# Gates by tanh instead of sigmoid, residual rows and channel norm moved to later steps, and a last LayerNorm shared by three engines, in a hybrid decoder layer

## The chip, the cores and the metric

One core of a Trainium2 chip runs the whole layer in one launch. The metric is the device time of that launch in microseconds (us). A run of the kernel before has a median of 1742.73 us over three runs (1742.01 to 1743.32).

The engines are named as in the profile: PE is the matrix engine (PEld its weight loads), DVE the vector engine, ACT the scalar engine, POOL the GpSimd engine, and SP the engine whose queue issues every DMA of this kernel (SPq). Each engine works through its own instructions in order and waits on the others by semaphores.

## The reference

A decoder layer on 256 tokens of width 2048, in float32:

```
x = LN1(alpha*x + 0.5*swiglu_ffn1(x))              # D_FF = 5632
u = x @ w_in + b_in                                # q 1024 | k 128 | v 128 | conv a 1024 | conv gate 1024
attn = sliding-window attention with sinks(q, k, v)   # 16 heads of 64, window 128
h = a * sigmoid(gate)
h = causal depthwise conv(h, 31 taps) + dw_b
conv = silu(LN_channels(h))
x = LN2(alpha*x + concat(attn, conv) @ w_out + b_out)
x = LN3(alpha*x + 0.5*swiglu_ffn2(x))
```

## The kernel before

Every matmul is done three times with split operands: a weight tile `raw` is rounded to `hi` by ACT (L113), and `lo = raw - hi` is made by DVE, in the middle of the program by POOL (L115). PE then adds `hi*hi`, `hi*lo` and `lo*hi` (L387 to L389). The class `Steps` streams the weights: `load` issues DMAs into four `raw` buffers, `split` makes `hi` and `lo` up to seven tiles ahead of PE, and `step()`, called after each bit of matmul work, runs the small jobs that are due. `st.at(delay, work, after)` puts a job on that list, so that the program order on each engine is set by these delays. `psA` has two PSUM buffers of two banks (tag `gu`) and `psB` four of one bank (tag `acc`).

The program runs FFN 1, the mixer, and FFN 2.

- **FFN** (`ffn`, L491): gate and up products by `token_group`, silu on ACT (L507), a transpose on DVE (L515), a split, and the down projection by `tokens_by` (L459). `tokens_by` goes through four column chunks `c` of 512 for two token blocks `b` of 128. `evacuate` (L262) adds a finished chunk to the residual `xt` on DVE (L265) and takes its statistics (L269). In the last six steps block 0 runs ahead: it is finished and normalised while PE still works for block 1.
- **Mixer** (`mixer`, L571): the input projection makes eight conv pairs (`c` in `ORDER`) and the queries (`q`). For a conv pair, `glu` (L660) takes the sigmoid of the gate on ACT (L663) and multiplies on DVE (L664) into `hc`. The 31 taps of the depthwise conv are DVE instructions (L655), started by one on ACT (L651); they accumulate in PSUM and end in `cv`. For each query tile, `attend` (L674) runs scores on PE (L680 to L684), maxima on DVE (L698 to L705), exponentials on ACT (L711, L715), the sum and its reciprocal on DVE (L718, L719), the division on ACT (L725), transposes on PE (L731), values on PE (L744) and the split of the result (L749 on ACT, L750 on DVE).
- **Residual rows** (`residuals`, L336): LayerNorm's gain and bias for the residual are applied to `xt` in four chunks. `get` issues the DMAs of the row vectors (L253). Two steps later ACT multiplies the bias row by alpha (L352), and the following steps hold the rest: DVE's L356, and L354, L360 and L361 on POOL in the mixer, on DVE in FFN 2.
- **Channel norm** (`channel_norm`, L779): when the conv is done, `conv_end` puts the transposes of `cv` (L785) for block 0, and a step later for block 1, into PE's queue, among the first half of the output projection. Then come the norm on DVE, transposes back (L803), silu on ACT (L808) and a split (L813, L814). The second half of the output projection needs these results.
- **The last norm** (`norm_to_rows`, L367): on DVE alone. Four instructions subtract the mean and multiply by the gain (L374), put between the short instructions of a reciprocal square root (`rsqrt`, L274: three rounds of L288 and L289), and four multiply by it and add the bias (L382). Each chunk is then stored (L563).

Of the kernel before, what the change touches and what calls it, by code (L numbers as in the profile page):

```python
# [9 lines left out]
F32 = mybir.dt.float32  # L10
# [3 lines left out]
AF = mybir.ActivationFunctionType  # L14
ALU = mybir.AluOpType
# [3 lines left out]
P = 128  # L19
D = 2048  # L20
S = 256
# [5 lines left out]
NC_ = D // 512  # L27
# [16 lines left out]
CONV_AT = (1, 3, 1)  # L44
# [135 lines left out]
def hybrid_layer(  # L180
# [3 lines left out]
    nc = tc.nc  # L184
# [5 lines left out]
    psA = ctx.enter_context(tc.tile_pool(name="psA", bufs=2, space=PSUM))  # L190
# [24 lines left out]
    xt = act.tile([P, 2, D], F32, tag="xt", name="xt")  # L215
# [21 lines left out]
    def load_constants():  # L237
# [5 lines left out]
        )  # L243
        nc.gpsimd.tensor_scalar(out=nsink, in0=psink, scalar1=-1.0, scalar2=None, op0=ALU.mult)

    def load_tokens(b):
        nc.sync.dma_start(xt[:, b], x[b * P : (b + 1) * P, :])
        st.at(4, lambda: nc.scalar.mul(xt[:, b], xt[:, b], ALPHA))
# [10 lines left out]
        if waiting:  # L259
            waiting.pop(0)()  # L260

    def evacuate(ps, b, c, factor, stats):  # L262

        y = xt[:, b, c * 512 : (c + 1) * 512]
        nc.vector.scalar_tensor_tensor(out=y, in0=ps, scalar=factor, in1=y, op0=ALU.mult, op1=ALU.add)  # L265
# [70 lines left out]
    def residuals(par, row, more, eng, start, every):  # L336

        def scale():
            for b in range(2):
                nc.vector.tensor_scalar(  # L340
                    out=par[:, b, 3:4], in0=par[:, b, 2:3], scalar1=ALPHA, scalar2=None, op0=ALU.mult
                )

        st.at(start, scale)
        for c in range(NC_):
            at = start + 1 + c * every

            def get(c=c, at=at):
                g, be = row_chunk(row, c, f"rg{row}_{c}"), row_chunk(row + 1, c, f"rb{row}_{c}")
                bo = row_chunk(more, c, f"ro{row}_{c}") if more is not None else None  # L350
                ys = [xt[:, b, c * 512 : (c + 1) * 512] for b in range(2)]
                work = [lambda: nc.scalar.mul(be, be, ALPHA)]  # L352
                if more is not None:
                    work.append(lambda: eng.tensor_tensor(out=be, in0=be, in1=bo, op=ALU.add))  # L354
                for b in range(2):
                    work.append(lambda b=b: nc.vector.tensor_scalar(  # L356
                        out=ys[b], in0=ys[b], scalar1=par[:, b, 0:1], scalar2=par[:, b, 3:4],
                        op0=ALU.subtract, op1=ALU.mult,
                    ))
                    work.append(lambda b=b: eng.tensor_tensor(out=ys[b], in0=ys[b], in1=g, op=ALU.mult))  # L360
# [6 lines left out]
    def norm_to_rows(b, stats, par, gb, store):  # L367

        mv, r = par[:, b, 0:2], par[:, b, 2:3]
        nc.vector.bn_aggr(out=mv, in_=stats[b].rearrange("p c s -> p (c s)"))  # L370

        def scaled(c):
            y = xt[:, b, c * 512 : (c + 1) * 512]
            nc.vector.scalar_tensor_tensor(  # L374
                out=y, in0=y, scalar=mv[:, 0:1], in1=gb[c][0], op0=ALU.subtract, op1=ALU.mult
            )

        scaled(0)
        rsqrt(mv[:, 1:2], r, [lambda c=c: scaled(c) for c in range(1, NC_)])
        for c in range(NC_):  # L380
            y = xt[:, b, c * 512 : (c + 1) * 512]
            nc.vector.scalar_tensor_tensor(out=y, in0=y, scalar=r, in1=gb[c][1], op0=ALU.mult, op1=ALU.add)  # L382
            store(b, c, y)


    def mm3(ps, s_hi, s_lo, m_hi, m_lo, start, stop):
# [69 lines left out]
                        evacuate(sums[b], b, c, factor, None)  # L456
                    st.step(1.36)

    def tokens_by(lhs, k0, nk, factor, stats, finish):  # L459

        half = nk // 2
        order = [(c, t) for c in range(NC_) for t in range(half)]
        skew = SKEW if finish is not None else 0
        held, sums = [], {}
        for n, (c, t) in enumerate(order):
            if t == 0:
                sums[c] = [psB.tile([P, 512], F32, tag="acc", name=f"acc{b}") for b in range(2)]
            w = st.take()
            token_mm(sums[c][0], lhs, k0, t, nk, 0, w)
            if t == half - 1:  # L470
                evacuate(sums[c][0], 0, c, factor, stats)
            if n >= len(order) - skew:
                held.append((c, t, w))
            else:
                token_mm(sums[c][1], lhs, k0, t, nk, 1, w)
                st.release()
            if t == half - 1 and not held:
                evacuate(sums[c][1], 1, c, factor, stats)
            if n == len(order) - 1 and skew:
                finish(0)  # L480
            st.step()
        for n, (c, t, w) in enumerate(held):
            token_mm(sums[c][1], lhs, k0, t, nk, 1, w)
            st.release()
            if t == half - 1:
                evacuate(sums[c][1], 1, c, factor, stats)
            if n == skew - 1:
                finish(1)
            st.step()

    def ffn(xc, tag, skew, begun, prepare, finish):  # L491
        with tc.tile_pool(name=f"ffn{tag}", bufs=2) as pool:
            for part, (j0, j1) in enumerate(((0, JA), (JA, JT))):
                n = j1 - j0
# [36 lines left out]
                tokens_by((hh, hl), 0, n, 0.5, stats, (lambda b: finish(b, stats)) if part == 1 else None)  # L531

    def params(name):
        return small.tile([P, 2, 4], F32, tag=name, name=name, bufs=1)
# [16 lines left out]
    x2 = mixer(tc, nc, locals())  # L551


    rows3 = []

    def prepare3(pool):
        for c in range(NC_):
# [7 lines left out]
    ffn(  # L565
        x2, "2", SKEW, lambda: residuals(par2, 3, None, nc.vector, 4, 6), prepare3,
        lambda b, s: norm_to_rows(b, s, par3, rows3, store),
    )


def mixer(tc, nc, env):  # L571
# [6 lines left out]
    with tc.tile_pool(name="mix", bufs=1) as pool:  # L578
# [81 lines left out]
        def glu(i, ps):  # L660
            hc = hcs[i % HB]
            sg = pool.tile([P, S], F32, tag="sg", name="sg", bufs=2)
            nc.scalar.activation(sg, ps[:, S:], AF.Sigmoid, bias=bias[:, 18 + i : 19 + i])  # L663
            nc.vector.scalar_tensor_tensor(  # L664
                out=hc[:, CK - 1 :], in0=ps[:, :S], scalar=bias[:, 10 + i : 11 + i], in1=sg,
                op0=ALU.add, op1=ALU.mult,
            )
            st.vector(0.4, 2.2)
            todo.append((i, hc))
# [244 lines left out]
```

## Time and profile before

| what | value |
|---|---|
| median of three runs | 1742.73 us |
| the profiled execution's own time | 1742.81 us |
| its span, from the first to the last instruction | 1740.9 us |
| mean granted PE clock | 0.997 |
| instructions | 22193 |
| PE busy | 1716.7 us, 99% |
| DVE, ACT, POOL busy | 1197.8, 802.5, 199.7 us |
| HBM traffic over the span | 192 GB/s |

The busy shares are averages over stages with different limits. PE is busy nearly all the time, so that the time can only change where PE stands still or where nothing of PE is left: ahead of its first matmul, in its few waits, and behind its last matmul. A row of the timeline gives the start, the duration, the engine, the line, the operation with its tiles, and, in brackets, how long the engine had stood idle and who released it.

### The profile page before, as it was taken

What the parts mean: (1) busy time and instruction counts of PE and PEld (TensorE: products, weight loads), DVE (VectorE), ACT (ScalarE), POOL (GpSimd) and SP (SyncE); (2) the same over time, 40 slices, a digit from 0 to 9 for tenths busy, and PEclk for the clock granted to TensorE, in tenths of its full rate; (3) what the DMA queues carried; (4) which work ended last, traced back from release to release, by engine and by line L of the source; (5) the groups of instructions that cost most, each with busy time, mean ns of one, the idle gap of its engine ahead of it and who ended that gap; (6) DMA issues with size and microseconds to landing.
All of it is one profiled execution on the core that took longest, in us unless ns stands there. A gap on an engine that the chain in (4) does not pass through costs nothing.

```text
span 1740.9 us, 22193 instructions
## 1 busy us (share of the span) xinstructions
PE 1716.7 (99%) x8198; PEld 1436.1 (82%) x8198; DVE 1197.8 (69%) x1954; ACT 802.5 (46%) x1024; POOL 199.7 (11%) x109
## 2 busy tenths in 40 slices
PE   8999999999999999999999999999999999999996
PEld 6888888888888888898997888888888888888885
DVE  6877776446777765638898588887764467777655
ACT  5544444334444443567565473444443344444430
POOL 0000000000000000178887300000000000000000
PEclk9999999999999999999999999999999999999999
DMA  8865655665565556464554556665556555555761
GB/s 275 282 201 194 192 194 189 198 194 195 192 193 194 193 187 200 146 197 147 175 167 163 194 189 210 208 227 193 192 184 204 193 195 193 192 194 195 232 204 61
DMA packets 96301, 336.42 MB, mean 193 GB/s; under 512 B 11200, under 2 KB 11840, under 8 KB 95936
## 3 DMA queue, kind: packets, MB, share of 16 engines
q1 hardware_dynamic: 96192, 335.00, 58.9%
q8 instruction: 64, 1.05, 0.2%
q14 instruction: 45, 0.37, 0.1%
HBM read 332.86 MB, written 2.10 MB: 192 GB/s over the span
## 4 chain that ended last, share of the span: by engine, by line
PE 88%; DVE 7%; ACT 2%; DMA 1%; issue 1%; POOL 0%; SPq 0%; DVEq 0%; ACTq 0%; POOLq 0%
PE grp L388 18%; PE grp L387 18%; PE grp L389 18%; PE acc L387 10%; PE acc L389 10%; PE acc L388 10%; DVE conv L655 4%; DMA rb<-in_rows 1%; PE grp L406 1%; PE grp L408 0%; PE grp L409 0%; POOL lo L115 0%; DVE xt L356 0%; PE tp L301 0%; ACT pr L725 0%
## 5 line engine op out<-in xcount | busy, mean ns | idle before, releaser
L113 ACT CAST hi<-raw 128x1024 fp32r<-128x1024 f32 (+1 forms) x614 | 639.7, 1047 | 747.8 <-PE grp L389 332.0
L115 DVE TENSOR_TENSOR lo<-raw,hi 128x1024 fp32r<-128x1024 f32 (+1 forms) x542 | 660.7, 1224 | 391.8 <-ACT hi L113 387.4
L387 PE MATMUL grp<-hi,xcat 128*128 128x512 f32 x1392 | 542.9, 390 | 5.7 <-ACT hi L113 5.7
L388 PE MATMUL grp<-lo,xcat 128*128 128x512 f32 x1392 | 542.8, 390 | 0.0
L389 PE MATMUL grp<-hi,xcat 128*128 128x512 f32 x1392 | 542.5, 390 | 0.0
L387 PEld LDWEIGHTS grp<-hi,xcat 128*128 128x128 f32 x1392 | 261.9, 188 | 60.4 <-ACT hi L113 6.0
L388 PEld LDWEIGHTS grp<-lo,xcat 128*128 128x128 f32 x1392 | 261.9, 188 | 55.1 <-DVE lo L115 0.9
L389 PEld LDWEIGHTS grp<-hi,xcat 128*128 128x128 f32 x1392 | 261.9, 188 | 54.4
L387 PE MATMUL acc<-hi,hh 128*128 128x512 f32 x704 | 274.0, 389 | 0.0
L389 PE MATMUL acc<-hi,hl 128*128 128x512 f32 x704 | 273.9, 389 | 0.0
L388 PE MATMUL acc<-lo,hh 128*128 128x512 f32 x704 | 273.9, 389 | 0.0
L115 POOL TENSOR_TENSOR lo<-raw,hi 128x1024 fp32r<-128x1024 f32 x72 | 171.9, 2409 | 772.2 <-ACT hi L113 766.4
L515 DVE STREAM_TRANSPOSE hf<-ht 32x128 f32<-32x128 f32 x704 | 212.7, 302 | 11.3
L389 PEld LDWEIGHTS acc<-hi,hl 128*128 128x128 f32 x704 | 132.2, 188 | 27.5
L387 PEld LDWEIGHTS acc<-hi,hh 128*128 128x128 f32 x704 | 132.2, 188 | 27.3
L388 PEld LDWEIGHTS acc<-lo,hh 128*128 128x128 f32 x704 | 132.2, 188 | 27.3
L655 DVE SCALAR_TENSOR_TENSOR conv<-hc,cw_sb,conv 128x256 f32<-128x256 f32 x232 | 106.9, 486 | 8.7 <-ACT conv L651 3.9
L387 PE MATMUL in_c<-xcat,hi 128*128 128x256 f32 x256 | 73.9, 289 | 0.0
L388 PE MATMUL in_c<-xcat,hi 128*128 128x256 f32 x256 | 72.4, 283 | 0.0
L389 PE MATMUL in_c<-xcat,lo 128*128 128x256 f32 x256 | 72.4, 283 | 0.0
L265 DVE SCALAR_TENSOR_TENSOR xt<-acc,xt 128x512 f32<-128x512 f32 x48 | 33.1, 690 | 55.2 <-PE acc L389 55.2
L507 ACT ACTIVATE sl<-grp 128x256 f32<-128x256 f32 x88 | 32.9, 383 | 48.7 <-PE grp L389 48.7
(118 smaller groups left out, 1058.6 us busy)
## 6 DMA issues: line engine op xcount, KB each, us to landing
raw<-in_wu SPq DMA_DIRECT2D x350, 512.0 KB, 4.6
raw<-in_wd SPq DMA_DIRECT2D x176, 512.0 KB, 4.6
raw<-in_win SPq DMA_DIRECT2D x52, 512.0 KB, 4.2
raw<-in_wout SPq DMA_DIRECT2D x32, 512.0 KB, 4.4
xt<-in_x SPq DMA_DIRECT2D x2, 1024.0 KB, 8.5
rg<-in_rows SPq DMA_DIRECT2D x8, 256.0 KB, 5.3
rb<-in_rows SPq DMA_DIRECT2D x8, 256.0 KB, 6.6
out<-xt SPq DMA_DIRECT2D x8, 256.0 KB, 2.8
```

Source lines behind the costliest of these rows:

```text
L113: nc.scalar.copy(hi, raw)
L115: eng.tensor_tensor(out=lo, in0=raw, in1=hi.bitcast(F32), op=ALU.subtract)
L265: nc.vector.scalar_tensor_tensor(out=y, in0=ps, scalar=factor, in1=y, op0=ALU.mult, op1=ALU.add)
L387: nc.tensor.matmul(ps, s_hi, m_hi, start=start, stop=False)
L388: nc.tensor.matmul(ps, s_hi, m_lo, start=False, stop=False)
L389: nc.tensor.matmul(ps, s_lo, m_hi, start=False, stop=stop)
L406: nc.tensor.matmul(ps, lhs[1][at], w[0][:, n], start=False, stop=k == nk - 1)
L507: nc.scalar.activation(sl, ps[b][:, : JG * P], AF.Silu)
L515: nc.vector.transpose(dst[:, t], src[:, f])
L655: nc.vector.scalar_tensor_tensor(out=acc if k < CK - 1 else cv[:, i], in0=hc[:, k : k + S], scalar=cw_sb[:, i, k : k + 1], in1=acc, op0=AL ...
```

## The change

1. **Gates.** `glu` used one ACT instruction with Sigmoid. It now uses two: Tanh of half the gate, and an Identity that adds 1. The missing factor 0.5 goes into the taps `cw_sb`, and the gate's bias is halved too, both once at the start, on POOL.
2. **Residual rows.** The work on the rows starts five steps after their DMAs are issued, not two. The DMAs stay where they were. This holds for the mixer and for FFN 2.
3. **Channel norm.** Both blocks' channel norms are put one step later.
4. **The last norm.** For token block 1, the chunks 1 to 3 stay in PSUM after `evacuate`, which writes them where it read them; chunks 1 and 2 get a `psA` buffer for that. For block 1, chunk 0 is handled by ACT (subtract the mean, later multiply by the reciprocal root) and POOL (times the gain, later plus the bias). DVE does chunks 1 and 2 as before, and chunk 3 after them. Block 0 is unchanged.

```diff
+        nc.gpsimd.tensor_scalar(out=bias[:, 18:], in0=bias[:, 18:], scalar1=0.5, scalar2=None, op0=ALU.mult)
+        nc.gpsimd.tensor_scalar(out=cw_sb, in0=cw_sb, scalar1=0.5, scalar2=None, op0=ALU.mult)
...
-    def evacuate(ps, b, c, factor, stats):
+    def evacuate(ps, b, c, factor, stats, stay=False):
-        y = xt[:, b, c * 512 : (c + 1) * 512]
-        nc.vector.scalar_tensor_tensor(out=y, in0=ps, scalar=factor, in1=y, op0=ALU.mult, op1=ALU.add)
+        x_ = xt[:, b, c * 512 : (c + 1) * 512]
+        y = ps if stay else x_
+        nc.vector.scalar_tensor_tensor(out=y, in0=ps, scalar=factor, in1=x_, op0=ALU.mult, op1=ALU.add)
...
-                    st.at(2 + n, x_, True)
+                    st.at(5 + n, x_, True)
...
-        scaled(0)
-        rsqrt(mv[:, 1:2], r, [lambda c=c: scaled(c) for c in range(1, NC_)])
-        for c in range(NC_):
-            y = xt[:, b, c * 512 : (c + 1) * 512]
-            nc.vector.scalar_tensor_tensor(out=y, in0=y, scalar=r, in1=gb[c][1], op0=ALU.mult, op1=ALU.add)
-            store(b, c, y)
+        if b == 0:
+            scaled(0)
+            rsqrt(mv[:, 1:2], r, [lambda c=c: scaled(c) for c in range(1, NC_)])
+        else:
+            nc.vector.tensor_scalar(out=par[:, b, 3:4], in0=mv[:, 0:1], scalar1=-1.0, scalar2=None, op0=ALU.mult)
+            nc.scalar.activation(ys[0], ys[0], AF.Identity, bias=par[:, b, 3:4])
+            nc.gpsimd.tensor_tensor(out=ys[0], in0=ys[0], in1=gb[0][0], op=ALU.mult)
+            rsqrt(mv[:, 1:2], r, [lambda c=c: scaled(c) for c in (1, 2)])
+            nc.scalar.mul(ys[0], ys[0], r)
+            nc.gpsimd.tensor_tensor(out=ys[0], in0=ys[0], in1=gb[0][1], op=ALU.add)
+        for c in range(NC_) if b == 0 else (1, 2, 0, 3):
+            if b == 1 and c == 3:
+                scaled(3)
+            if b == 0 or c > 0:
+                nc.vector.scalar_tensor_tensor(
+                    out=ys[c], in0=ins[c], scalar=r, in1=gb[c][1], op0=ALU.mult, op1=ALU.add
+                )
+            store(b, c, ys[c])
...
-            nc.scalar.activation(sg, ps[:, S:], AF.Sigmoid, bias=bias[:, 18 + i : 19 + i])
+            nc.scalar.activation(sg, ps[:, S:], AF.Tanh, bias=bias[:, 18 + i : 19 + i], scale=0.5)
+            nc.scalar.activation(sg, sg, AF.Identity, bias=1.0)
...
-            channel_norm(0)
-            st.at(CONV_AT[2], lambda: channel_norm(1))
+            st.at(1, lambda: channel_norm(0))
+            st.at(1 + CONV_AT[2], lambda: channel_norm(1))
```

The order of ACT's instructions early in the mixer, around the second query tile's exponentials (`pr`), was this in the kernel before; `rb` is the bias row that L352 multiplies, and `ACT_TABLE_LOAD` loads the table of the function that follows:

```order
L113 CAST hi_6181<-raw_6001 128x1024
L352 ACTIVATE rb_0_6082<-rb_0_6082 128x512
L711 ACT_TABLE_LOAD
L711 ACTIVATE pr,sm<-sc,nm 128x128
L711 ACTIVATE pr,sm<-sc,nm 128x256
L711 ACTIVATE pr,sm<-sc,nm 128x128
L711 ACTIVATE pr,sm<-sc,nm 128x256
L715 ACTIVATE sc<-sk 128x2x2
```

At the same place of the changed kernel, whose lines have other numbers (L740 is the exponentials, L744 the sink's), ACT has these:

```order
L113 CAST hi_6184<-raw_6003 128x1024
L740 ACTIVATE pr,sm<-sc,nm 128x128
L740 ACTIVATE pr,sm<-sc,nm 128x256
L740 ACTIVATE pr,sm<-sc,nm 128x128
L740 ACTIVATE pr,sm<-sc,nm 128x256
L744 ACTIVATE sc<-sk 128x2x2
```

The row's instruction stands 18 places further on, and the table load is gone. Over the whole program ACT has 13 table loads before and 4 now.

At the end of the program DVE's instructions for block 1 were these, from the third L374 on (`par` holds the mean and the reciprocal root, `g` and `b` are rows of gain and bias):

```order
L374 SCALAR_TENSOR_TENSOR xt<-xt,par_121,g_13527 128x512
L288 TENSOR_SCALAR rs_t<-par_121,rs_w 128x1
L289 TENSOR_SCALAR par_121<-rs_t,par_121 128x1
L374 SCALAR_TENSOR_TENSOR xt<-xt,par_121,g_13531 128x512
L288 TENSOR_SCALAR rs_t<-par_121,rs_w 128x1
L289 TENSOR_SCALAR par_121<-rs_t,par_121 128x1
L382 SCALAR_TENSOR_TENSOR xt<-xt,par_121,b_13521 128x512
L382 SCALAR_TENSOR_TENSOR xt<-xt,par_121,b_13525 128x512
L382 SCALAR_TENSOR_TENSOR xt<-xt,par_121,b_13529 128x512
L382 SCALAR_TENSOR_TENSOR xt<-xt,par_121,b_13533 128x512
```

In the changed kernel they are these (L379 is the old L374, L292 and L293 the old L288 and L289, L398 the old L382):

```order
L379 SCALAR_TENSOR_TENSOR acc_13938<-acc_13938,par_121,g_13537 128x512
L292 TENSOR_SCALAR rs_t<-par_121,rs_w 128x1
L293 TENSOR_SCALAR par_121<-rs_t,par_121 128x1
L292 TENSOR_SCALAR rs_t<-par_121,rs_w 128x1
L293 TENSOR_SCALAR par_121<-rs_t,par_121 128x1
L398 SCALAR_TENSOR_TENSOR xt<-acc_13752,par_121,b_13535 128x512
L398 SCALAR_TENSOR_TENSOR xt<-acc_13938,par_121,b_13539 128x512
L379 SCALAR_TENSOR_TENSOR acc_14122<-acc_14122,par_121,g_13541 128x512
L398 SCALAR_TENSOR_TENSOR xt<-acc_14122,par_121,b_13543 128x512
```

Two of the eight long instructions have left DVE, the third round of the root has nothing between its instructions, and the last two long instructions depend on each other.

More of the change, by code (lines that the diff above doesn't have):

```diff
@@ L466, in tokens_by @@
             if t == 0:
-                sums[c] = [psB.tile([P, 512], F32, tag="acc", name=f"acc{b}") for b in range(2)]
+                sums[c] = [psB.tile([P, 512], F32, tag="acc", name="acc0")]
+                if kept is not None and c in (1, 2):
+                    sums[c].append(psA.tile([P, 2, 512], F32, tag="gu", name="acc1")[:, 0])
+                else:
+                    sums[c].append(psB.tile([P, 512], F32, tag="acc", name="acc1"))
+                if kept is not None and c > 0:
+                    kept[1, c] = sums[c][1]
             w = st.take()
@@ L551, in hybrid_layer @@
     x2 = mixer(tc, nc, locals())
-    rows3 = []
+    rows3, kept = [], {}
     def prepare3(pool):
```

20 lines of the change are left out of this document (11 added, 9 removed).

## The prediction

> **What bounds the kernel now.** I read the page first, then PE's waits, then the timeline around each of them. The page says that PE is busy for all but 24 us of the span:
>
> ```profile
> span 1740.9 us, 22193 instructions
> PE 1716.7 (99%) x8198; PEld 1436.1 (82%) x8198; DVE 1197.8 (69%) x1954; ACT 802.5 (46%) x1024; POOL 199.7 (11%) x109
> ```
>
> So only those 24 us can be won. PE's waits, whole program, give where they lie (total, times, longest):
>
> ```profile
> PE grp L387 <- ACT hi L113: 5.7, 1, 5.7
> PE tp L731 <- ACT pr L725: 1.8, 2, 1.6
> PE acc L387 <- DVE hc L664: 1.5, 1, 1.5
> PE sc L680 <- DVE ml L750: 0.5, 1, 0.5
> PE tp L301 <- DVE z L317: 0.4, 1, 0.4
> PE tk L785 <- DVE cv L655: 0.3, 1, 0.3
> ```
>
> The first is the start, which the change leaves alone, and L301 belongs to a norm that it leaves alone. The other four lie in the mixer and are 1.8 + 1.5 + 0.5 + 0.3 = 4.1 us. No other wait of PE exists, for weights neither. What is left is the tail. PE's last matmul and DVE's work for block 1 behind it, from the timeline:
>
> ```profile
> 1727.10 0.39 PE L389 MATMUL acc<-hi,hl 128*128 128x512 f32 x1
> ...
> 1728.15 0.68 DVE L265 SCALAR_TENSOR_TENSOR xt<-acc,xt 128x512 f32<-128x512 f32 x1
> ...
> 1729.60 0.26 DVE L370 BATCH_NORM_AGGREGATE par<-st 128x2 f32<-128x24 f32 x1
> 1729.89 0.75 DVE L374 SCALAR_TENSOR_TENSOR xt<-xt,par,g 128x512 f32<-128x512 f32 x1
> 1730.56 0.15 DVE L279 TENSOR_SCALAR rs_v<-par 128x1 f32<-128x1 f32 x1
> ...
> 1730.81 0.14 DVE L284 TENSOR_SCALAR rs_w<-rs_v 128x1 f32<-128x1 f32 x1
> 1730.87 0.74 DVE L374 SCALAR_TENSOR_TENSOR xt<-xt,par,g 128x512 f32<-128x512 f32 x1
> ...
> 1731.96 0.74 DVE L374 SCALAR_TENSOR_TENSOR xt<-xt,par,g 128x512 f32<-128x512 f32 x1
> 1732.62 0.27 DVE L288 TENSOR_SCALAR rs_t<-par,rs_w 128x1 f32<-128x1 f32 x1
> 1732.93 0.21 DVE L289 TENSOR_SCALAR par<-rs_t,par 128x1 f32<-128x1 f32 x1
> ...
> 1734.27 2.74 DVE L382 SCALAR_TENSOR_TENSOR xt<-xt,par,b 128x512 f32<-128x512 f32 x4
> ```
>
> PE is done at 1727.49. DVE, still on block 0's norm, takes block 1's last chunk at 1728.15 and ends at 1734.27 + 2.74 = 1737.01; the last store and the closing take the remaining 3.9 us to 1740.9. This stretch is DVE's alone.
>
> **The mixer: gates and rows.** Why does PE wait there? Its longest wait, 1.6 us for L725, is behind this stretch of ACT:
>
> ```profile
> 780.33 0.63 ACT L352 ACTIVATE rb<-rb 128x512 f32<-128x512 f32 x1 [4.29 <-DMA rb<-in_rows]
> 780.96 1.28 ACT L711 ACT_TABLE_LOAD   x1
> ...
> 785.05 1.49 ACT L725 ACTIVATE pr<-pr,sm 128x128 f32<-128x128 f32 x4
> 786.56 1.28 ACT L663 ACT_TABLE_LOAD   x1
> 787.85 0.47 ACT L663 ACTIVATE sg<-in_c,bias 128x256 f32<-128x256 f32 x1
> ```
>
> ACT stands in front of a row that is still on its way, and behind it in the queue are the exponentials, the division, the weights' `hi` and the gate. DVE shows the same hole from its side, and the wait for the first out-projection buffer at its end:
>
> ```profile
> 778.45 0.17 DVE L705 TENSOR_SCALAR sk<-sk 128x4 f32<-128x4 f32 x1
> ...
> 784.21 0.16 DVE L718 TENSOR_TENSOR sm<-sc,sm 128x4 f32<-128x4 f32 x1 [4.68 <-ACT sc L715]
> ...
> 788.36 0.48 DVE L664 SCALAR_TENSOR_TENSOR hc<-in_c,bias,sg 128x256 f32<-128x256 f32 x1 [1.30 <-ACT sg L663]
> ...
> 903.58 0.48 DVE L664 SCALAR_TENSOR_TENSOR hc<-in_c,bias,sg 128x256 f32<-128x256 f32 x1 [1.49 <-ACT sg L663]
> ...
> 915.55 0.48 DVE L664 SCALAR_TENSOR_TENSOR hc<-in_c,bias,sg 128x256 f32<-128x256 f32 x1
> ```
>
> With the row three steps later, the exponentials start when their maxima are there: L705 ends at 778.62, so they run from 778.65 instead of 780.96 + 1.28 = 782.24, 3.6 us earlier, and L718 comes 3.6 us earlier too. The weights' cast and the division follow at once and end near 782.9. The gate then has no table load ahead of it, but a second instruction behind it. That one isn't in the trace; the nearest rows are the gate itself (0.47 us, the same shape) and L352 (0.63, twice the elements), so it costs 0.3 to 0.5 us, and I take 0.4. By these steps `hc` starts at 783.7 instead of 788.36, 4.7 us earlier, and the `hc` at 903.58, which waits for another gate with a load ahead of it, wins up to 1.28 - 0.4 = 0.9 us more.
>
> That the lead is kept and not lost again is the assumption of this step. DVE's waits between 776 and 916 speak for it:
>
> ```profile
> DVE hc L664 <- ACT sg L663: 6.3, 4, 2.0
> DVE sm L718 <- ACT sc L715: 6.2, 4, 4.7
> DVE conv L655 <- ACT conv L651: 1.9, 2, 1.0
> ```
>
> It waits for ACT alone, never for PE: it is a queue that lags behind PE, and keeps what it is given until it has caught up. Then it waits for PE, which is harmless. At the end of this stretch PE waits 1.5 us for the `hc` at 915.55, whose gate had its input long before:
>
> ```profile
> 911.91 0.47 ACT L663 ACTIVATE sg<-in_c,bias 128x256 f32<-128x256 f32 x1 [3.12 <-PE in_c L389]
> ```
>
> In the changed kernel PE is there 1.8 + 0.5 = 2.3 us earlier, so that wait would be 1.5 + 2.3 = 3.8 us if DVE stayed where it was. It needs a lead of 3.8 us; it has 4.7 at 788 and some 0.9 more at 903. The gate's own path (PE's input at 909.6, then 0.47 + 0.4 + 0.48) ends at 911.0, 1.1 us ahead of PE's need at 912.1. The waits for L750 and L725 fall away by the same lead. The fourth, 0.3 us at L785, falls away because the transposes stand one step later. The step also moves the chain behind them, up to block 1's splits, which the output projection's second half needs. Before, these splits (L814) ended at 958.2, and the first half ended at 961.5, where L265 waits for its last matmul:
>
> ```profile
> 955.43 2.75 DVE L814 TENSOR_TENSOR ml<-sw,mh 128x512 fp32r<-128x512 f32 x2 [2.99 <-ACT mh L813]
> ...
> 961.51 0.69 DVE L265 SCALAR_TENSOR_TENSOR xt<-acc,xt 128x512 f32<-128x512 f32 x1 [2.03 <-PE acc L389]
> ```
>
> A step there is twelve matmuls of 0.226 us (884 in 200 us, in a row further down), 2.7 us. PE's part of the chain comes 2.7 - 4.1 = 1.4 us earlier than before in all, so the splits end at 956.8. PE needs the first of them six matmuls into the second half, at 961.5 - 4.1 + 1.4 = 958.8, the second 5.4 us later. That cover of 2 us hides the step. If it were gone, each further us would be one of PE; two more waits of DVE for one POOL add (1.29 each, L360's row below) would show 0.6 us. I take 0. The three extra steps of the rows also move L356, L354, L360 and L361 on DVE and POOL; POOL does the same adds, and their reader is the output projection's L265, behind all query tiles; each us by which it were late would hold back a PSUM buffer of PE by as much. I take 0. In FFN 2 PE has no wait that the same edits could remove: 0. The two POOL instructions at the start lie before any POOL work: 0. Sum for the mixer: -4.1 us, between -4.1 (no wait left) and 0 (all of them come back elsewhere).
>
> **The tail.** DVE's new order, with durations from the rows above. The negated mean starts at 1729.89 and takes 0.06 of issue (L284 to the next row); the root's start 0.31, so the first long instruction starts at 1730.26. A round with one long instruction is 1.09 us (1730.87 to 1731.96), so the next starts at 1731.35, and its round's L289 ends at 1732.53. The third round has no cover: 0.31 + 0.21 and 0.02, so the root is ready at 1733.07 (before: 1734.25). Then two long ones at 2.74 / 4 = 0.685 each, chunk 3's first at 1734.47, and its second only when that is finished, 0.75 + 0.02 later: 1735.24, done at 1735.99. That is 1.0 us ahead of 1737.01.
>
> These instructions have PSUM where they had SBUF. The nearest rows are the taps that write PSUM and the last tap, which writes SBUF; the others show a short DVE instruction in the stretch where POOL works, and one of POOL's own:
>
> ```profile
> L655 DVE SCALAR_TENSOR_TENSOR conv<-hc,cw_sb,conv 128x256 f32<-128x256 f32 x232 | 106.9, 486 | 8.7 <-ACT conv L651 3.9
> L655 DVE SCALAR_TENSOR_TENSOR cv<-hc,cw_sb,conv 128x256 f32<-128x256 f32 x8 | 3.8, 478 | 0.1
> L705 DVE TENSOR_SCALAR sk<-sk 128x4 f32<-128x4 f32 x8 | 10.3, 1293 | 0.3
> L360 POOL TENSOR_TENSOR xt<-xt,rg 128x512 f32<-128x512 f32 x8 | 10.3, 1292 | 0.0
> ```
>
> The taps are 8 ns apart: PSUM costs nothing here. [...]
>
> Chunk 0 goes beside: mean at 1730.04, ACT 0.63 to 0.75 us (L352's row, and more for its operand), POOL 1.29, ACT again when the root is there (1733.1 to 1733.9), POOL 1.29: ready at 1735.3 with two hand-offs of 0.1, 0.7 us before chunk 3, behind which its store no longer matters. Sum for the tail: -1.0 us, from +0.3 (POOL holds DVE, below) to -1.1.
>
> **The sum.** 1740.9 - 4.1 - 1.0 = 1735.8 us of span. The profiled execution took 1742.81, 1.9 more than its span and 0.08 more than the median: 1735.8 + 1.9 = **1737.7 us**, 0.29% less. About 0.2% (3.5 us) is what a measurement of this kernel can tell from no change.
>
> **Rivals.**
> *A. One wait stays.* DVE's lead is eaten where DVE has to wait for PE, and the out projection's first buffer still comes 1.6 us late. For it: the need (3.8) and the lead (4.7) are close. 1739.3 us, on the edge of 0.2%.
> *B. POOL holds DVE in the tail.* L705, four elements wide, took 1293 ns in the stretch where POOL works, as long as one of POOL's adds, and only 0.17 at 778.45. If the tail's instructions were held like that for one POOL add, the tail would win 1.0 - 1.3, nothing: 1739.0 us with the mixer's gain. Against it: the 232 taps ran in the same stretch at 486 ns each. [...]
> *C. The mixer's waits come back.* DVE and not PE sets the mixer's pace, so that a shorter ACT only moves PE's waits to the next buffer. For it: DVE never waits for PE between 776 and 916, in the rows quoted above. Only the tail is won: 1741.8 us, no change.
> *D. Slower: the clock.* A PE without pauses is granted less clock. 1% of it is 17 us; it decides from a mean of 0.992 down, where 8.6 us (5.1 + 3.5) are lost: 1746.3 us and more. Against it, this stretch of the windows (start and end, length, the busy time of PE, PEld, DVE, ACT and POOL, and then the granted clock):
>
> ```profile
> 200.00:400.00 200.00, 200.00 (x884) 165.62 (x883) 117.84 (x156) 82.25 (x86) 0.00 (x0) 1.00 0.60 194
> ```
>
> 200 us without a pause keep 1.00.
>
> **How the numbers follow.** The forecast gets 0.50, A 0.20, B 0.10, C 0.16, D 0.04. Faster by over 0.2% are the forecast, B and half of A: 0.70. Within 0.2%: half of A and C: 0.26. Slower: 0.04. The range goes from 1736.6 (the forecast with the 0.4 us of L301 gone too, and 0.7, by which the fastest of the three runs lies under their median) to 1741.2, which holds the forecast, A and B with as much spread, and leaves out C and D, 0.20.
>
> **What would show it.** In the changed kernel PE's waits should be the start and L301 alone, ACT should have 4 table loads and no wait of the rows' multiplication for its DMA in the mixer, the `hc` that stood at 788.36 should come near 784, and DVE should end 8.5 us behind PE's last matmul instead of 9.5. A new wait of PE of over 1 us between 780 and 970 would make it wrong (A or C), as would a long instruction of the tail above 1 us (B).

## The result, and the profile after

The changed kernel takes 1731.17 us in the median of four runs (1730.11 to 1732.39), against 1742.37 for the kernel before (1741.99 to 1743.32): a ratio of 0.9935, with a 95% interval of 0.9918 to 0.9952. That is 11.2 us, 0.65%, faster (8.4 to 14.3 us by the interval). The forecast was 1737.7 us in a range of 1736.6 to 1741.2: the sign was right, and the gain was more than twice what was forecast. The profiled execution took 1730.11 us. Its page begins:

```profile
span 1728.3 us, 22205 instructions
PE 1709.9 (99%) x8198; PEld 1433.8 (83%) x8198; DVE 1200.3 (69%) x1953; ACT 798.3 (46%) x1025; POOL 203.8 (12%) x113
```

PE has the same 8198 instructions as before, but its busy time fell from 1716.7 to 1709.9 us. So 6.8 us of what the page called busy weren't needed for the work: they were matmuls at a lowered clock, and pauses that overlapping records hide (both below). PE's waits, whole program, are as forecast, the start and L305 (the old L301) alone:

```profile
PE grp L405 <- ACT hi L113: 5.5, 1, 5.5
PE tp L305 <- DVE z L321: 0.4, 1, 0.4
```

**Where the 12.6 us of span went.** Three places can be parted by landmarks on PE: the first transpose behind FFN 1, and the last matmul. First the two transposes, before and after:

```profile
724.50 0.71 PE L301 MATMUL tp<-ident,z 128*128 128x128 f32 x5
```

```profile
722.84 0.38 PE L305 MATMUL tp<-ident,z 128*128 128x128 f32 x2
```

The changed kernel is 1.66 us ahead there, where the change does nothing; the same landmark lay between 722.84 and 725.28 in the ten profiles of kernels with this start, so this is the luck of one execution: PE's granted clock first rose to 1.00 at 12.09 us before and at 8.87 after, and half of that difference is 1.6 us. From there to the last matmul PE took 1727.10 - 724.50 = 1002.60 us before and 1715.43 - 722.84 = 992.59 after: 10.0 us less, where 4.1 were forecast. From the last transposes of the mixer on (1016.52 and 1004.83) to the last matmul it is 710.58 and 710.60, so FFN 2 gave nothing and all 10.0 us lie in the mixer. The rest is the tail. DVE behind PE's last matmul, in the changed kernel:

```profile
1716.48 0.69 DVE L269 SCALAR_TENSOR_TENSOR acc<-acc,xt 128x512 f32<-128x512 f32 x1
...
1718.62 0.75 DVE L379 SCALAR_TENSOR_TENSOR acc<-acc,par,g 128x512 f32<-128x512 f32 x1
...
1721.47 1.41 DVE L398 SCALAR_TENSOR_TENSOR xt<-acc,par,b 128x512 f32<-128x512 f32 x2
1722.80 0.75 DVE L379 SCALAR_TENSOR_TENSOR acc<-acc,par,g 128x512 f32<-128x512 f32 x1
1723.58 0.75 DVE L398 SCALAR_TENSOR_TENSOR xt<-acc,par,b 128x512 f32<-128x512 f32 x1
```

and PE's last matmul, ACT's and POOL's part beside it:

```profile
1715.43 0.39 PE L407 MATMUL acc<-hi,hl 128*128 128x512 f32 x1
```

```profile
1721.53 0.72 ACT L392 ACTIVATE xt<-xt,par 128x512 f32<-128x512 f32 x1 [2.38 <-DVE par L293]
```

```profile
1722.33 1.27 POOL L393 TENSOR_TENSOR xt<-xt,b 128x512 f32<-128x512 f32 x1 [1.84 <-ACT xt L392]
```

DVE ends at 1724.33, 8.51 us behind the end of PE's last matmul (1715.82), where it was 9.52. In all, 1.66 + 10.0 + 1.0 = 12.7 us, to 0.1.

**The view that had been left out.** PE's waits are those of its matmuls. The weight loads (PEld) have a list of their own. In the kernel before it is, for the mixer:

```profile
PEld tp L731 <- ACT pr L725: 5.1, 14, 1.8
PEld acc L387 <- DVE hc L664: 1.9, 1, 1.9
...
PEld L680 <- issue: 0.7, 2, 0.5
PEld tk L785 <- DVE cv L655: 0.6, 1, 0.6
```

The matmuls' list had 1.8, 1.5, 0.5 and 0.3 at these places. The difference is largest at the transposes L731: besides the long wait there are thirteen short ones, because each of the division's four pieces on ACT releases only its own transposes. They look like this around the long wait, on PEld:

```profile
785.50 0.14 PEld L731 LDWEIGHTS tp<-ident,pr 128*128 128x128 f32 x1 [1.83 <-ACT pr L725]
785.90 0.43 PEld L731 LDWEIGHTS tp<-ident,pr 128*128 128x128 f32 x3 [0.26 <-ACT pr L725]
786.59 0.20 PEld L731 LDWEIGHTS tp<-ident,pr 128*128 128x128 f32 x2 [0.26 <-ACT pr L725]
```

A matmul's record is longer than the time until the next one can start (0.39 us against 0.227 for 512 columns, 0.28 against 0.12 for 256), so that the records of a paced series close up to a busy line, by up to 0.16 us at each matmul. In the changed kernel the same places have this left:

```profile
PEld tp L760 <- issue: 0.3, 2, 0.2
PEld L709 <- issue: 0.2, 1, 0.2
PEld tp L760 <- ACT conv L679: 0.2, 1, 0.2
```

So 8.3 us of idle weight loads became 0.7. The second thing that PE's list doesn't show stands in the windows of the kernel before (busy times of PE, PEld, DVE, ACT and POOL, then the granted clock):

```profile
783.00:786.00 3.00, 1.30 (x10) 0.91 (x9) 1.68 (x5) 2.97 (x11) 0.72 (x1) 1.00 0.24 94
786.00:789.00 3.00, 2.93 (x16) 2.65 (x17) 1.63 (x5) 2.97 (x5) 2.88 (x2) 0.65 0.07 16
789.00:792.00 3.00, 3.00 (x22) 3.00 (x22) 2.89 (x8) 3.00 (x7) 2.61 (x2) 0.78 0.47 161
```

Behind the long wait PE is busy but at a lowered clock, with 16 and 22 matmuls in 3 us where the changed kernel has 27 and 30:

```profile
783.00:786.00 3.00, 3.00 (x27) 3.00 (x27) 3.00 (x9) 2.41 (x4) 2.29 (x2) 1.00 0.52 169
786.00:789.00 3.00, 3.00 (x30) 2.87 (x31) 3.00 (x9) 2.14 (x3) 2.90 (x2) 1.00 0.48 152
```

The clock's part is (1 - 0.65 + 1 - 0.78) x 3 = 1.7 us; by the trace it stood at 0.50 from 786.92 to 790.33. Together 7.6 + 1.7 = 9.3 of the 10.0 us. The distances between the starts of PE's matmuls assign all of it, as the mixer has the same pairs of neighbours in both kernels. Of the 10.0 us, 5.5 lie at the transposes behind the division (2.2 ahead of the first ones, 3.3 between them), 1.8 in the output projection around its wait for `hc`, 1.5 between the query matmuls at the lowered clock, 0.6 ahead of the scores and 0.55 at the channel norm's transposes.

### The profile page after: what moved, and what is told of

It is laid out like the page before. It is cut to its first block, busy times and chain, and to the rows that moved or that the text cites. A ratio compares the mean times of both kernels' runs of the same rounds, so it can differ in the third digit from the quotient of the medians.

```text
span 1728.3 us, 22205 instructions
## 1 busy us (share of the span) xinstructions
PE 1709.9 (99%) x8198; PEld 1433.8 (83%) x8198; DVE 1200.3 (69%) x1953; ACT 798.3 (46%) x1025; POOL 203.8 (12%) x113
## 4 chain that ended last, share of the span: by engine, by line
PE 98%; DVE 2%; DMA 0%; issue 0%; ACT 0%; SPq 0%; DVEq 0%
PE grp L406 18%; PE grp L405 18%; PE grp L407 18%; PE acc L405 11%; PE acc L407 11%; PE acc L406 11%; PE in_c L405 2%; PE in_c L406 2%; PE in_c L407 2%; PE in_q L405 1%; PE in_q L406 1%; PE in_q L407 1%; PE grp L424 1%; PE grp L426 1%; PE grp L427 1%; PE tp L773 0%
## 5 line engine op out<-in xcount | busy, mean ns | idle before, releaser
L542 DVE STREAM_TRANSPOSE hf<-ht 32x128 f32<-32x128 f32 x704 | 212.8, 302 | 11.2
```

The lines of the kernel that those rows point to most:

```text
L542: nc.vector.transpose(dst[:, t], src[:, f])
```

## The experiments

The theory formed from these rows (theory 1) is that the mixer's loss was the idle weight loads and the lowered clock behind the long wait, not the listed waits. The rivals were that only listed waits count and the rest came from another part of the change or from the start (theory 2), and, for single steps, those in the texts below. "Stretch" is the time from the first transpose behind FFN 1 to PE's last matmul in the profiled execution: it leaves out the start and the tail.

| kernel | ratio to before, 95% interval | stretch, us | against before |
|---|---|---|---|
| before | 1 | 1002.60 | |
| changed | 0.9935, 0.9918 to 0.9952 | 992.59 | -10.0 |
| rows alone (e1_rows) | 0.9976, 0.9967 to 0.9985 | 998.87 | -3.7 |
| gates alone (e2_gates) | 0.9971, 0.9960 to 0.9983 | 997.15 | -5.4 |
| channel norm alone (e3_channel) | 1.0000, 0.9991 to 1.0009 | 1002.55 | 0.0 |
| last norm alone (e4_tail) | 0.9997, 0.9988 to 1.0006 | 1002.13 | -0.5 |
| all but the last norm (m_tail) | 0.9954, 0.9942 to 0.9966 | 992.57 | -10.0 |
| rows alone, L356 on ACT (e5_rows_act) | 0.9972, 0.9961 to 0.9982 | 995.92 | -6.7 |
| changed, with warm-up (w_warm) | 0.9942, 0.9929 to 0.9956 | 992.58 | -10.0 |

**The four parts alone.** Each is one part of the diff on the kernel before. Rows alone:

```diff
-                    st.at(2 + n, x_, True)
+                    st.at(5 + n, x_, True)
```

> The kernel before with the residual rows used five steps after their DMAs and nothing else. Theory 1 (hidden waits): the mixer's loss is the idle time of PE's weight loads (5.1 us ahead of L731, 1.9 at L664, and smaller ones, 8.4 us in all against 4.1 that PE's own waits list) and 1.7 us of lowered clock behind the long wait at 784. The rows alone remove the ACT wait of 4.29 us at 780, so the wait of 1.8, the 0.5 of the pieces behind it and the lowered clock go (4.0 us), and by DVE's lead some of what follows: 5 to 7 us faster, PEclk 1.00 all through the mixer. Theory 2 (listed waits): only PE's listed waits count, and the rest of the 11.2 us lies in other parts or in the varying start: 1.6 to 4.1 us faster.

It measured 1737.65 us against 1742.04, 4.4 faster. The wait at L731 is gone, but PE has a new one:

```profile
PE sc L680 <- DVE ml L750: 2.2, 1, 2.2
```

and the clock falls behind that one instead:

```profile
799.00:801.00 2.00, 0.22 (x1) 0.10 (x1) 1.93 (x5) 0.00 (x0) 2.00 (x2) 0.89 0.46 164
801.00:807.00 6.00, 6.00 (x28) 4.84 (x27) 4.28 (x14) 4.86 (x15) 2.07 (x2) 0.50 0.91 187
```

The clock stood at half from 800.54 to 807.37, which costs 3.4 us beside the wait. So the forecast of a clock of 1.00 all through was wrong, and the gain lies below theory 1's 5 to 7 us; theory 2's 1.6 to 4.1 would fit the time, but not the rows. DVE came late to L750 here because one L356 took 2.67 us, on DVE, while POOL had started a subtraction 0.03 us before it:

```profile
794.59 2.67 DVE L356 TENSOR_SCALAR xt<-xt,par 128x512 f32<-128x512 f32 x1
```

```profile
794.56 2.41 POOL L115 TENSOR_TENSOR lo<-raw,hi 128x1024 fp32r<-128x1024 f32 x1
```

Gates alone are the gate's two ACT lines and the two POOL lines of the diff.

> The kernel before with the Tanh gates and nothing else. Theory 1: the exponentials at 782.26 come 1.3 us earlier, so 0.5 of the wait of 1.8 stays and the row's DMA still stops ACT; the lowered clock goes if the stretch with little PE work is short enough; the gates behind it come 0.9 us earlier each and most of the later idle weight loads (0.9 at 850, 0.9 at 892, 0.7 at 901, 1.9 at 914) go: 4 to 8 us faster. Theory 2: 1.3 of the 1.6 and part of the 1.5 at L664: 2 to 3 us faster.

1736.66 us, 5.4 faster (3.0 to 7.0 by the interval), and the stretch says 5.4 too, where the listed waits allow 2 to 3: theory 2 falls here. PE's longest wait moves to the same place as with the rows alone, and this one left the clock at 1.00:

```profile
PE sc L684 <- DVE ml L754: 1.7, 1, 1.7
```

Channel norm alone and last norm alone:

```diff
-            channel_norm(0)
-            st.at(CONV_AT[2], lambda: channel_norm(1))
+            st.at(1, lambda: channel_norm(0))
+            st.at(1 + CONV_AT[2], lambda: channel_norm(1))
```

> The kernel before with the channel norms one step later and nothing else. Theory 1: the 0.6 us of idle weight loads ahead of L785 go: 0.3 to 0.6 us faster. Theory 2: 0.3 us. A rival by which the later chain is late for the output projection's second half would be slower by over 0.5 us. A gain above 1 us speaks against both theories.

> The kernel before with the last norm shared by three engines and nothing else. Both theories: 1.0 us faster, as DVE ends 8.5 us behind PE's last matmul instead of 9.5; PE's part is unchanged. A gain above 2 us would mean that part of the 11.2 us came from here.

The channel norm gave 1742.26 us, no change (the listed 0.3 us went, and the interval is too wide for it). The last norm gave 1741.36 us; the ratio can't tell that from none, but its profile can: DVE ends at 1735.57 + 0.75 = 1736.32, 8.52 us behind PE's last matmul at 1727.80. By the stretch, rows and gates alone give 3.7 + 5.4 = 9.1 us and both together, with the channel norm, 10.0. Each alone leaves a wait for `ml` that isn't there with both. In the medians this difference can't be seen: 4.4 + 5.4 = 9.8 us alone, 8.4 us together (the next run).

**All but the last norm.** The changed kernel with `norm_to_rows` and `evacuate` of before.

> The changed kernel with the last norm as before, so the gates, rows and channel norm alone. By the profile the tail is worth 1.0 us: 1732.2 us, 9.9 to 10.2 us faster than before. If the parts overlap, less; if the last norm helps more than DVE's end shows, it would be slower than 1733.

1732.62 us against 1741.02 for the kernel before in that job, 8.4 faster (5.9 to 10.1 by the interval), where 9.9 to 10.2 were expected; the expected time, 1732.2 us, was met to 0.4. Its stretch is 992.57, the changed kernel's to 0.02, and DVE ends 9.52 us behind the last matmul. By the profile, the last norm's 1.0 us and the mixer's 10.0 us don't overlap.

**What held DVE in the rows alone.** L356 as one ACT instruction, with its bias from a short DVE instruction per block:

```diff
...
+                nc.vector.tensor_scalar(
+                    out=nb[:, b], in0=par[:, b, 0:1], scalar1=par[:, b, 3:4], scalar2=-1.0, op0=ALU.mult, op1=ALU.mult
+                )
...
-                    work.append(lambda b=b: nc.vector.tensor_scalar(
-                        out=ys[b], in0=ys[b], scalar1=par[:, b, 0:1], scalar2=par[:, b, 3:4],
-                        op0=ALU.subtract, op1=ALU.mult,
-                    ))
+                    work.append(lambda b=b: nc.scalar.activation(
+                        ys[b], ys[b], AF.Identity, scale=par[:, b, 3:4], bias=nb[:, b]
+                    ))
...
```

> The kernel before with the rows five steps after their DMAs, as in the kernel with the rows alone, and the residual's first instruction (L356) as one ACT instruction, with its bias from one short DVE instruction more per block. In the kernel with the rows alone one L356 took 2.67 us, until POOL's instruction ended that had started 0.03 us before it, and PE waited 2.2 us for L750 behind it, with 6.75 us of half clock after that. Theory 1 (DVE held by POOL, then the clock): 2 to 5 us faster than the rows alone, 1733 to 1736 us, and no long wait at L680. Rival (DVE lags there by its taps in any case): the wait stays above 1 us and the time within 1 us of the rows alone, 1737 to 1738 us.

The wait at L680 is gone from the profile, the clock is 1.00 throughout, and the stretch is 2.95 us shorter than with the rows alone. The median, 1736.52 us against 1740.92, is 4.4 us faster than before, no more than the rows alone were, so that theory 1's 2 to 5 us weren't won in the median. The profiled execution of the rows alone took 1739.38 us, the longest of its eleven runs (1736.39 to 1739.38). So the rows show that one L356 took 2.67 us in that execution, that PE waited 2.2 us for DVE behind it, and that its clock stood at half for 6.83 us; how often this happens, and what it costs in the median, stays open.

**What a pause of PE costs.** The changed kernel with a pause behind 42 gate groups of the FFNs. ACT copies `n_` pieces of the group's result; PE transposes the last one in FFN 1, and each as it comes in FFN 2. The result isn't used.

```diff
...
+                        for q in range(n_):
+                            nc.scalar.copy(zp[:, q % 4 * P : (q % 4 + 1) * P], ps[1][:, q % 4 * P : (q % 4 + 1) * P])
+                            if tag == "2" or q == n_ - 1:
+                                nc.tensor.transpose(pz[:, 0, q % 4 * P : (q % 4 + 1) * P], zp[:, q % 4 * P : (q % 4 + 1) * P], ident)
...
```

> The changed kernel with a pause of PE put behind 42 of the FFNs' gate groups, 20 us apart: ACT copies 2, 3, 4, 5, 6, 8 or 12 pieces of the group's result, and PE transposes the last piece (FFN 1) or each piece as it comes (FFN 2), a result that nobody reads. It measures what a pause of PE costs by its length. Theory 1 (clock by window): below some 1.5 us a pause costs itself, above some 4 us the clock always falls to 0.50 for 3 to 7 us, so that 1.5 to 3.5 us more are lost, and between the two it depends on when the pause falls; in FFN 2, with transposes between the pieces, the clock falls no less often, and PE's own waits list less than the time that is lost, by 0.1 to 0.2 us a piece. Theory 2 (a pause costs what is listed): the granted clock stays at 1.00 behind all pauses below 4 us and the time lost is the sum of PE's listed waits within 10%.

1801.23 us, 70.1 more than the changed kernel. The lists have

```profile
PE pz L539 <- ACT zp L537: 34.6, 42, 3.3
```

```profile
PEld pz L539 <- ACT zp L537: 48.5, 41, 2.6
PEld pz L539 <- issue: 3.7, 1, 3.7
```

so PE's shows half of what was lost, and PEld's 52.2 us, three quarters. Two pauses with twelve pieces tell why. In FFN 1:

```profile
653.15 0.39 PE L408 MATMUL grp<-hi,xcat 128*128 128x512 f32 x1
655.77 0.33 PE L539 MATMUL pz<-ident,zp 128*128 128x128 f32 x1 [2.23 <-ACT zp L537]
655.85 0.48 PE L406 MATMUL acc<-hi,hh 128*128 128x512 f32 x1
```

In FFN 2:

```profile
1675.38 0.39 PE L408 MATMUL grp<-hi,xcat 128*128 128x512 f32 x1
1676.12 2.21 PE L539 MATMUL pz<-ident,zp 128*128 128x128 f32 x12 [0.36 <-ACT zp L537]
1678.09 0.48 PE L406 MATMUL acc<-hi,hh 128*128 128x512 f32 x1
```

From the last matmul's start plus 0.227 to the next one's start the hole is 2.47 and 2.48 us; listed are 2.23 and 0.36. Added up in this way the 42 holes are 61.7 us, and the matmuls behind them lose another 6.5 (0.11 behind each, 1.7 at half pace once). Of the 1.9 us that are left, the start can hold all: the clock first rose at 13.59 us here, against 8.87 in the changed kernel's profile. Theory 2 falls, theory 1's "0.1 to 0.2 us a piece" holds.

The clock was the surprise: none of the 20 holes of up to 2.48 us in FFN 1 lowered it; the only longer one, of 3.55 us, did. So longer holes were tried, with 12 to 36 pieces.

> The pause kernel again with 12, 15, 18, 21, 25, 30 and 36 pieces, so with holes of some 2.5, 3.0, 3.5, 4.0, 4.7, 5.5 and 6.5 us in PE's work; in the kernel before it, 41 holes of up to 2.48 us lowered nothing and one of 3.55 us was followed by 9 matmuls at 0.43 us. Theory 1 (window): from 3.4 us on more and more of the holes, from 6.8 us all of them, are followed by 3 to 4 us at half pace, which costs 1.5 to 2 us each; between 2.5 and 3.4 us some. In FFN 2, where PE transposes a piece every 0.17 us in the hole, that bit of work keeps the clock up if the window counts any work, and doesn't if it counts work done: then they fall as often as in FFN 1. Theory 2 (the clock falls by the idle time alone, at a fixed length): one length parts all holes with from all holes without.

These are two windows of that kernel around a hole of 2.97 us that ends at 600.16:

```profile
597.00:600.00 3.00, 0.34 (x2) 0.00 (x0) 0.00 (x0) 2.62 (x16) 0.00 (x0) 1.00 0.55 190
600.00:604.00 4.00, 3.92 (x11) 3.14 (x12) 3.09 (x7) 1.52 (x4) 0.00 (x0) 0.59 0.05 14
```

And two of the mixer. There the same pause was put behind the first half of each input projection group, and in a second kernel three more pieces behind each, with two transposes that wait for each (the last four lines, in the second kernel alone):

```diff
             features(ps[:, :S])
...
+            for q in range(n_):
+                nc.scalar.copy(zp[:, q % 2 * P : (q % 2 + 1) * P], ps[:, q % 2 * P : (q % 2 + 1) * P])
+            nc.tensor.transpose(ps[:, S : S + P], zp[:, :P], ident)
+            for q in range(3):
+                nc.scalar.copy(zp[:, S:], ps[:, :S])
+                for h in range(2):
+                    nc.tensor.transpose(ps[:, S : S + P], zp[:, S + h * P : S + (h + 1) * P], ident)
```

> The changed kernel with a pause of PE behind the first half of each of the 14 input projection groups in the mixer: ACT copies 8, 10 or 12 pieces of the result and PE transposes one of them, which nobody reads. In FFN 1 holes of up to 2.48 us never lowered the clock (0 of 20), of 3.0 us and more nearly always (19 of 20); in the mixer of the kernel before and of two variants the clock fell behind holes of 1.9 to 2.6 us. Theory 1 (the place matters): of holes of 1.8 to 2.5 us between the mixer's matmuls of 256 columns some are followed by half pace. Theory 2 (the length of the hole alone): none is, and the clock fell in the mixer for the slow transposes or scores behind the hole.

> The same with 6, 8 or 10 pieces, and behind the hole three more pieces of 256 columns, each with two transposes that wait for it, as the division's pieces stood behind the long wait at 784 in the kernel before. Theory 1 (the place matters): the clock falls as often as in the kernel without the pieces, or less often, since in FFN 2 transposes each 0.17 us kept it up in holes of 6.6 us (0 of 21). Theory 2 (hole and slow transposes together): it falls behind most of them here, and behind none in the kernel without the pieces.

All four pause kernels together, a hole counted as "lowered" where the granted clock falls to 0.50 in it or right behind it (holes as above; in the mixer up to the first transpose):

| place | hole, us | lowered |
|---|---|---|
| FFN 1, matmuls of 512 columns | 0.77 to 2.48 | 0 of 22 |
| FFN 1 | 2.97 to 3.55 | 6 of 7 |
| FFN 1 | 4.00 to 6.59 | 13 of 13 |
| FFN 2, a transpose every 0.17 us in the hole | 0.77 to 6.59 | 0 of 42 |
| mixer, matmuls of 256 columns | 1.70 | 0 of 5 |
| mixer | 2.05, 2.38 | 4 of 9 |
| mixer, then three pieces some 1 us apart | 1.36 to 2.05, 4.3 to 5.6 with the pieces | 12 of 14 |

A fall cost 1.5 to 2.8 us in FFN 1, beyond the hole. The first kernel of the mixer took 1767.26 us, the second 1818.61.

By this table holes of 2.05 us lower the clock in the mixer and none of up to 2.48 us does in FFN 1. But the place isn't the reason, as the instants of the falls, which each trace records, show. In each execution all falls and rises of the granted clock lie a whole number of 3.4133 us apart, to 0.02 us (from the first rise on 227, 1 and 276 of them in the kernel before, 501 in the changed kernel): in these traces the clock changes only at the ends of windows of that length, which go on through holes and work alike. What parts the holes is how much of one lies in one window. The first mixer kernel has two holes of 2.04 us that show it. The one from 774.70 to 776.74 is cut at 775.22 by a window's end, the one from 810.28 to 812.33 lies in one window. For each, this is the window that holds most of it, and the next one:

```profile
775.22:778.64 3.42, 1.89 (x16) 1.90 (x17) 3.25 (x9) 2.35 (x11) 0.00 (x0) 1.00 1.01 185
778.64:782.05 3.41, 3.41 (x31) 3.41 (x30) 0.65 (x4) 3.38 (x11) 2.40 (x1) 1.00 0.70 181
```

```profile
809.36:812.77 3.41, 1.53 (x14) 1.32 (x13) 3.20 (x10) 3.39 (x15) 3.40 (x2) 1.00 1.00 273
812.77:816.18 3.41, 3.41 (x19) 3.41 (x18) 2.41 (x8) 2.23 (x10) 2.38 (x1) 0.50 0.73 211
```

The same holes of FFN 1 and of the first mixer kernel, by the longest part that lies in one window (holes up to the transpose that ends them):

| place | longest part in one window, us | lowered |
|---|---|---|
| FFN 1 | up to 1.92 | 0 of 23 |
| FFN 1 | 1.98 to 3.41 | 19 of 19 |
| mixer, first kernel | 1.25 to 1.70 | 0 of 10 |
| mixer, first kernel | 2.04 to 2.38 | 4 of 4 |

This parts them all, and the two places agree: in these runs the limit lies between 1.92 and 1.98 us. The hole of 3.49 us in FFN 1 that lowered nothing has 1.74 us in one window and 1.66 in the next. So both theories of the mixer are wrong: neither the place nor the length alone decides. Where a hole of 2 to 3.9 us (an estimate: up to twice that limit) falls in its window is luck. In the rows alone, 2.08 us of the wait lay in one window and the clock fell; in the gates alone, 0.47 and 1.35 us lay in two and it didn't. Theory 2 of the longer holes, one length that parts them, falls too: 2.97 us lowered the clock where 3.49 didn't. Theory 1's lengths of 3.4 and 6.8 us, the author's estimate, aren't the limits either: from 2.97 to 3.55 us 6 of 7 holes lowered it, and from 4.00 us on all 13. The half clock lasted one window, or two where 0.94 us or more of the hole reach into the window behind (7 of 7 in FFN 1; 0 of 12 where it is 0.37 or less).

The three pieces of the second mixer kernel make the clock fall with less of a hole: two transposes every microsecond were too little work in a window behind holes of 1.36 to 2.05 us, 12 times of 14. The wait of the kernel before at 784 is of that kind. The window that ends at 786.92 holds 1.8 us of hole and, behind it, 1.1 us of transposes that wait for the division, and there the clock fell. How much work in a window is enough isn't settled, and the windows were found in the traces of runs that were made for other questions.

**The start.** The changed kernel with 13 matmuls of zeros ahead of the first real one:

```diff
...
+    for _ in range(13):
+        nc.tensor.matmul(wps[:, 0], wb[:, :P], wb[:, :512], start=True, stop=True)
```

> The changed kernel with 13 bf16 matmuls of zeros ahead of PE's first real matmul, into a PSUM buffer that nobody reads. The start's matmuls at 0.43 us, until 8.63 in the changed kernel's profile and 11.98 in that of the kernel before, are a lowered clock behind an idle PE by theory 1: then the real ones run at 0.227 us from the first or soon after, 1.5 to 3 us are won against the changed kernel (1728 to 1730 us) and the runs lie closer together. If the slow start is set by the first weights instead, nothing is won (1731 us).

1730.71 us (1730.50 to 1731.04): within the measurement of the changed kernel, so the expected 1.5 to 3 us weren't won, though the runs lie closer together. The real matmuls do run at 0.23 us from the second on, where those of the changed kernel took 0.43 us until 8.63 and its granted clock first rose to 1.00 at 8.87: so the slow start is a lowered clock:

```profile
1.46 5.14 PE L225 MATMUL wps<-warm 128*128 128x512 bf16 x13 [1.46 <-DVE warm L221]
6.25 0.58 PE L411 MATMUL grp<-hi,xcat 128*128 128x512 f32 x1
6.66 0.40 PE L412 MATMUL grp<-lo,xcat 128*128 128x512 f32 x1
...
13.53 0.50 PE L412 MATMUL grp<-lo,xcat 128*128 128x512 f32 x1 [0.76 <-DVE lo L115]
```

But what they win they wait for later: by 13.53 PE has caught up with the weights, while the DMA engines are busy all the time (a mean busy share of 0.99 to 1.03 from 8 to 14 us). By the runs (1730.11 to 1732.39 us without the warm-up, 1730.50 to 1731.04 with it), an estimate, the changed kernel's luckier executions lose nothing at the start that the warm-up could win; the unlucky ones lose up to some 2 us.

## Why the prediction was wrong, step by step

- **"So only those 24 us can be won."** This is the step that failed. It took PE's busy row for work. The row said 99%, 6.8 us of it went away with the same instructions, and in the pause kernel PE's waits listed 34.6 us of 70.1. PEld's 82% would not have shown the loss either, as the stretch without a pause from 200 to 400 us has 83% (165.62 of 200 us); its waits, 8.3 us in the mixer, do.
- **The mixer's term, -4.1 us.** The mechanism was right and the size was not. The four waits went, as forecast; with the smaller pauses that the list doesn't show, and the lowered clock, they had cost 10.0 us: 7.6 of idle weight loads, 1.7 of lowered clock, and 0.7 that only the distances between starts show. The rival about the clock looked the other way: it feared less clock without pauses, and it was the pauses that lowered it.
- **Exponentials and `hc` earlier.** Right, and by some 1.4 us more than forecast: the prediction left the maxima where they were, but the first gate had lost its table load too, and its `hc` and DVE's work behind it came 1.3 us earlier (766.63 + 1.66 = 768.3 against 769.60). With the 1.66 us of the start added, the exponentials begin at 775.48 + 1.66 = 777.1 (forecast 778.65) and `hc` at 780.61 + 1.66 = 782.3 (783.7; before 788.36). The gate's second instruction takes 0.42 us (forecast 0.4):

```profile
775.48 0.37 ACT L740 ACTIVATE pr<-sc,nm 128x128 f32<-128x128 f32 x1 [1.10 <-DVE sk L731]
...
779.67 0.45 ACT L691 ACTIVATE sg<-in_c,bias 128x256 f32<-128x256 f32 x1
780.16 0.42 ACT L692 ACTIVATE sg<-sg 128x256 f32<-128x256 f32 x1
```

- **DVE's lead is kept (against rivals A and C).** Right for the whole change: PE has no wait left in the mixer. It was closer than it looked, since with the rows alone or the gates alone a wait of 2.2 or 1.7 us appears some 15 us later.
- **Channel norm, FFN 2, residual rows: 0.** Right. The channel norm alone gave a ratio of 1.0000, and FFN 2 takes 710.58 and 710.60 us. L356 on DVE beside POOL is the one that might have cost something.
- **The tail, -1.0 us.** Right: 8.51 us behind PE, forecast 8.5. Long instructions on PSUM take 0.75 us as they did on SBUF, so the tail won its 1.0, and none took longer beside POOL's two of 1.26 and 1.27 us, so rival B falls. Chunk 0 is ready at 1723.60, 0.73 us before chunk 3 (forecast 0.7).
- **The sum.** With the right term it is 1740.9 - 10.0 - 1.0 = 1729.9 of span and 1731.8 us, 0.6 above the measured median.

## What to carry to other kernels

On an engine whose records overlap, read the waits of its weight loads and the distance between starts, and not the busy share: a gap shorter than the overlap (here 0.16 us at 512 columns) isn't seen, and a series that another engine paces looks like work. Price a pause of PE with what may follow it: look at the granted clock of the 3 us behind. In these runs it stood at half for 3.41 or 6.83 us, which cost half as much, where 1.98 us or more of the pause, or less with thin work behind it (12 of 14), lay in one window of 3.41 us. By that, an estimate, a pause of 2 to 3.9 us may or may not cost this, by where the window ends. And look at where the next wait goes when one part of a change is tried alone: with the rows or the gates alone PE waited for `ml` at a place where it waits for nothing with both.

## What the runs showed of the hardware

- The clock fell to half behind a pause, and stayed there for 3.41 us (the kernel before, 786.92 to 790.33) or twice that (6.83 us with the rows alone). In these traces it fell and rose only at the ends of windows of 3.413 us; 23 of 23 holes with at least 1.98 us in one window lowered it, and 0 of 33 with at most 1.92 us. By their whole length, holes of 2.97 us lowered it 3 times of 3 in FFN 1, and holes of 2.05 us 2 times of 5 in the mixer.
- A transpose every 0.17 us was enough work to keep the full clock through holes of 6.59 us.
- The same DVE instruction (L356, 128x512, eight times by 900 us with the rows alone) took 0.52 to 2.67 us, the longest time when a POOL subtraction had started 0.03 us before it; it ended 0.3 us behind that one. In the kernel before, five of its eight took 1.01 to 2.71 us, each until 0.28 or 0.29 us behind the end of a POOL instruction that ran when it began or started 0.01 us later; the other three took 0.52 to 0.54 us.
